# Transposing weights, queries and keys of a chunked-attention layer by 32x32 blocks and a trip through DRAM instead of by TensorE products

## The chip, the core and the metric

The kernel runs on one core of a Trainium2 chip. TensorE (PE) multiplies matrices, VectorE (DVE) and ScalarE (ACT) do the elementwise work, GpSimd (POOL) a few powers, and SyncE (SP) issues nearly all DMAs; 16 DMA engines move the bytes. The metric is device time in microseconds (us); lower is better. Each engine takes its instructions in the order in which the program lists them: an instruction that waits holds up those behind it on the same engine.

## What is computed

A model of four layers on 256 tokens of width 1024: a gated delta rule, an attention over one block, a retention layer, and, as the last, a chunked attention. Only the last, "layer D", is touched:

```python
proj = h @ w_in                                   # [256, 4 * 2048]
q, k, v, g = jnp.split(proj, 4, axis=-1)          # 16 heads of 128
q = rms_norm_f32(q.reshape(B, S, 16, 128), q_g)
k = rms_norm_f32(k.reshape(B, S, 16, 128), k_g)
...
s = einsum('bhqd,bhkd->bhqk', q_j, k_j) * scale + bias
p = softmax(where(valid, s, -1e30))
o = einsum('bhqk,bhkd->bqhd', p, v_j)
o = o * silu(g)
return o @ w_out
```

At 256 tokens each chunk of 64 queries sees all the chunks up to its own, so a head is one causal attention with a chunk-wise mask. All of it is float32.

## The kernel before

Weights come in units of [128, 1024] float32 (512 KB), one DMA each, into five `raw` buffers. ACT copies a unit to its first part `whi`, DVE subtracts it and gets the second part `wlo`; there are six pairs of parts. A product with split operands is three matmuls (hi·hi, hi·lo, lo·hi). `project_a` (L522) makes [128 tokens, 512 columns] twice, with four units of 12 matmuls of 512 columns; `project_b` (L501) makes [128 columns, 256 tokens] with a unit of 24 matmuls of 256 columns.

The order of the instructions is made on the host, when the program is built: `Tasks` (L269) runs each step of the work as a task with a priority, estimates what every operation takes, and issues the instructions in the order in which the engines would take them by these estimates. PE estimates are in `_cost_pe` (L237: 0.217 us for a split matmul of 512 columns); a DMA ends `DMA_LATENCY` = 2 us after its bytes have moved (L170, L353). On the chip, each engine then keeps that order, whatever things really take.

Layer D (`layer_d`, L1546) takes the units in the order `ORDER_D` (L157); q0 to q3 are the queries of four heads each, and so on for k, v and g (the gate); three gate units come ahead of all these. The pieces:

- `normed(name, q, reverse)` (L1590): after the projection, ACT squares and sums (eight instructions), POOL raises to the power -1/2, DVE scales into `xn` [128 tokens, 4 x 128]. For each half of the tokens PE then transposes four blocks of 128x128 by products with the identity (L1609), and ACT copies them to `qr` (reversed in order) or `kr`.
- `head(h)` (L1633) waits until its queries, keys, values and bias are there, then runs `attend` (L1108): scores on PE, softmax on DVE and ACT into `s`, three PE transposes of the weights (L1127), an ACT copy to `pT`, the product with the values, and an ACT copy to the output `or`. Heads have a priority (4.97) that goes before that of a projection (50 and more): their PE instructions are put between matmuls of projections as soon as the estimates have them ready.
- `gate(h)` (L1646) multiplies with 2 silu(g); `out_tile(n)` (L1679) makes 128 output columns each from 16 heads, adds them to `xT` and stores them.

PSUM has eight banks that the rings `PJ` (projections), `SS` (scores), `TT` (transposed weights), `OO` (outputs) and `MM` share. `hand_over(OO, TT)` (L1800) sets the shares of layer D: four for PJ, one each for SS, TT, OO and MM.

Of the kernel before, what the change touches and what calls it, by code (L numbers as in the profile page):

```python
# [10 lines left out]
F32 = mybir.dt.float32  # L11
# [9 lines left out]
P = 128  # L21
T = 256
D = 1024
# [3 lines left out]
# Per-partition columns: (name, number of columns)  # L27
# [12 lines left out]
# Constants that depend on shapes alone: (name, number of columns)  # L40
# [27 lines left out]
def _t5_hot():  # L68
    """[33, 384]: which bucket the relative position 255 - m falls in; the last row masks what lies ahead."""
    rel = 255 - np.arange(384)  # L70
    n = np.maximum(rel, 0)
    nf = np.maximum(n, 1).astype(np.float32)
    large = 16 + (np.log(nf / np.float32(16)) / np.float32(np.log(2048 / 16)) * np.float32(16)).astype(np.int32)
    bucket = np.where(n < 16, n, np.minimum(large, 31))
    hot = np.zeros((33, 384), np.float32)
    hot[bucket, np.arange(384)] = rel >= 0
    hot[32] = np.where(rel >= 0, 0.0, -1e30)
    return hot


def _decay():
    """[128 keys, 4 heads, 384]: key tile 0 with all queries, then key tile 1 with the last 128."""
# [29 lines left out]
def _plan():  # L112
    """The units of weights in the order of their use; those of the adaptive norms stand between the others."""
# [37 lines left out]
# Which units of weights are used whole, in float32 products  # L151
WHOLE = [("d_g", u) for u in (0,)] + [("a_qkv", u) for u in (0, 3, 4, 6, 7, 8, 9, 13, 14, 17, 18, 20, 22)]
# The order of the units
# [3 lines left out]
ORDER_D = "q1 k0 v0 q0 v2 g1 q2 k1 v1 q3 v3 g0 g3 k2 k3 g2".split()  # L157
ADA_FROM = ('a_z', 7)
ADA2_FROM = ('c_v', 3)
# Counts: units used before the norm, steps at once, units ahead, buffers  # L160
EARLY, BATCH, AHEAD, AHEAD2, FIRST_D, ADA_A, ADA2_EVERY = 1, 1, 1, 2, 3, 2, 1
RAWS, NPARTS, NKQ, NC, NVT = 5, 6, 3, 2, 2
# Priorities of tasks, the least goes first
# [4 lines left out]
# Estimates, in us  # L168
OVER, HOP, SAME = 0.03, 0.2, 0.1
DMA_LATENCY = 2.0  # L170
# [10 lines left out]
class Ring:  # L181
    """Free buffers: `b = yield ring` waits for one, ring.put(b) gives one back."""
# [22 lines left out]
class Engine:  # L205
    """Turns the calls of an engine into operations for a task to yield: (engine, estimated us, call, table)."""
# [57 lines left out]
def chain(*ops):  # L264
    """Operations of one engine, each on what the one before it made."""
    return [(e, c + SAME, f, t) for e, c, f, t in ops[:-1]] + [ops[-1]]


class Tasks:  # L269
    """Issues the instructions of concurrent tasks in the order in which the engines would take them.  # L270

    A task is a generator. It yields an operation or a list of operations of one engine, and goes on when they have
    ended by the estimates; a Ring, and gets a buffer; an Event, and waits for it; a number, its priority from there on
    (the least goes first)."""
# [59 lines left out]
    def dispatch(self, e):  # L334
# [18 lines left out]
        lat = DMA_LATENCY if e.startswith("D") else 0.0  # L353
# [5 lines left out]
        self.at(end + 1e-6, lambda: self.dispatch(e))  # the next operation of the same task may go first  # L359

    def hold(self, n):
        """While held, the vector and the scalar engine take nothing that can wait."""
        self.held += n
        if not self.held:
            for e in "VS":
                self.at(self.now, lambda e=e: self.dispatch(e))
# [10 lines left out]
def body(ctx, tc, a, out):  # L377
# [4 lines left out]
    dma, dma2 = Engine("D", nc.sync, _cost_dma), Engine("D2", nc.scalar, _cost_dma)  # L382

# [28 lines left out]
    nc.scalar.activation(phalf, nhalf, AF.Copy, scale=-1.0)  # the activation table is loaded meanwhile  # L412

    # PSUM: rings of whole banks; they change hands between the layers
# [22 lines left out]
    def h_set(i, name, wide=0):  # L437
        """Two float32r parts of transposed activations."""
# [10 lines left out]
    # ------------------------------------------------------------ weights: units of [128, 1024], in the order of use  # L449
# [11 lines left out]
    def unit(u):  # L461
        """One unit, whole or split exactly into two float32r parts; what belongs to the adaptive norms is summed at once."""
        raw = yield RAW
        src = a[u[0]][u[1]]
        if number[u] == 0:  # its first half is used before the other is there
# [35 lines left out]
    def project_b(units, x, x32, ps, ready):  # L501
        """[128 columns, tokens] of a product. x: (hi, lo) of the transposed activations, x32: the same, not split."""
# [19 lines left out]
    def project_a(name, q, x, pss, ready):  # L522
        """Two [128 tokens, 512 columns] of a product, with four units."""
# [32 lines left out]
    def sums_ops(ps, srcs):  # L556
        """Sums over the partitions of [128, 256] each, tokens on partitions: [128 tokens, 2, 96]."""
# [3 lines left out]
    def row_ops(ps, c):  # L561
        """A pair of token columns along the free dimension, on every partition."""
# [6 lines left out]
    # ------------------------------------------------------------ gated delta rule  # L569
    def layer_a(pool):  # L570
# [56 lines left out]
        def x_square(i):  # L627
            """Squares of two column tiles, added to those before."""
# [30 lines left out]
        def decays():  # L659
            """gg = -exp(a_log) softplus(a + dt_bias), beta = sigmoid(b), tokens on partitions"""  # L660
# [34 lines left out]
        def decay(h):  # L695
            """decay[s, c] = exp(sum of gg over s < m <= c), where the products of queries and keys will stand"""
# [16 lines left out]
        def conv(ch, dst):  # L713
            """dst [128, 256] = silu(conv) of channel tile ch."""
# [36 lines left out]
        def squared(h, x, dst):  # L751
            """Sums of the squares of the columns of x [128, 256]."""
# [7 lines left out]
        def norm_k(h, kq, done):  # L760
            """nk = the norm of the keys, bb = beta / nk ** 2"""
# [14 lines left out]
        def head(h):  # L776
            """The system matrices of head h and its squared norms."""
# [13 lines left out]
            # k.k of key tile 0 (256) and 1 (128), q.k of key tile 0 (256) and 1 (128)  # L791
# [10 lines left out]
            # the 16 x 16 diagonal blocks, side by side; then only what lies between blocks stays in MT  # L802
# [10 lines left out]
        def base(q):  # L813
            """V16 = (I + U)^-1 for the strictly upper 16 x 16 problems of four heads, block rows on partitions."""
# [31 lines left out]
        def gates(q):  # L846
            """zs = silu(z)"""
# [8 lines left out]
        # block solves: (I + B)^-1 = D (I - F)(I + F^2)(I + F^4), F = N D  # L856
# [54 lines left out]
        def outputs(t, q):  # L911
            """The outputs of four heads on one tile of tokens, their norm and gate, transposed in two parts."""
# [68 lines left out]
    def out_a(o_in, z_in, box, after):  # L981
        """The rows of the first four heads for all columns, then those of the others, two column tiles at a time."""
# [7 lines left out]
        # the two column tiles of a bank are one group, begun with zeros  # L990
# [35 lines left out]
    # ------------------------------------------------------------ from one layer to the next  # L1026
    class Next:
        """What the end of a layer makes for the next: scaled activations and sums of squares, a column tile at a time."""
# [24 lines left out]
        def squares(self, n):  # L1053
            """Adds to the sum; works on pairs, but for the last."""
# [22 lines left out]
        def weighted_squares(self, n, w):  # L1077
            """Adds to sums over the channels, tokens on partitions, with one weight of two for each half of the columns."""
# [11 lines left out]
    def ahead(u, nx, box):  # L1090
        """A product begun before its layer is, before norm and shift; box[u] = PSUM, with the product of the shift behind it."""
# [15 lines left out]
    # ------------------------------------------------------------ softmax attention of one head  # L1107
    def attend(A, kT, qT, bias, vv, o, half):  # L1108
        """o [128 dims, 256] = half times the output; queries stand reversed in their tile of 128 in qT and bias.

        x holds the negative scores, mx their least: minus the maximum of the scores."""
        ps = yield SS
        yield [pe.matmul(ps[:, :P], lhsT=qT[:, :P], rhs=kT[:, :P], start=True, stop=True),
               pe.matmul(ps[:, P:384], lhsT=qT[:, P:], rhs=kT, start=True, stop=True)]
# [11 lines left out]
        ps = yield TT  # L1126
        yield [pe.transpose(ps[:, i * P:(i + 1) * P], x[:, i * P:(i + 1) * P], ident) for i in range(3)]  # L1127
        A["s"].put(item)
        pT = yield A["pT"]
        yield s.activation(pT, ps[:, :384], AF.Copy)  # L1130
        TT.put(ps)
# [13 lines left out]
    def gate_out(o, zs, hi, lo):  # L1145
        """The two parts of o * zs."""
# [4 lines left out]
    # ------------------------------------------------------------ MoBA (one block of 256: causal attention within it)  # L1151
    def layer_b(pool, nx, begun, after):
# [16 lines left out]
        def biases():  # L1169
            """Rows of rel = 255 .. -127 for each head, then [128 - 1 - query, key]."""  # L1170
# [79 lines left out]
        def head(h):  # L1250
# [3 lines left out]
            yield from attend(A, K[h], Q[h], b_bias[:, h], [VV[q][:, t, hh * P:(hh + 1) * P] for t in range(2)], O[h], 1.0)  # L1254
# [43 lines left out]
    # ------------------------------------------------------------ adaptive norms  # L1298
    def cond(condb):
        """condb: silu(c) along the free dimension, on every partition"""  # L1300
# [4 lines left out]
    def ada(i, nx):  # L1305
        """mods[i] [128, 24]: shift, 1 + scale and gate of layer i as columns"""
# [11 lines left out]
    def modulate(hs, i, nx, k, r12, Y, r_in, done):  # L1318
        """hs = parts of rms_norm(x) * norm_g * (1 + scale) + shift"""
# [11 lines left out]
    def sixteen(pool, name, first):  # L1331
        """Two parts of [128, 16, 256], first: their first half."""
# [3 lines left out]
    # ------------------------------------------------------------ retention  # L1336
    def rope_tables(freq, sin, nsin, cos, done):
        """cos, sin and -sin of position * frequency, [128 frequencies, 256 tokens]"""
# [19 lines left out]
    def layer_c(pool, nx, first, sin, nsin, cos, rope_in, after, free):  # L1358
# [24 lines left out]
        def norm():  # L1383
            """The final norm (r1) and the norm of its result, together r12."""
# [501 lines left out]
```

## Time and profile before

| | us |
|---|---|
| median of 3 runs (801.78 to 802.7) | 802.01 |
| the profiled execution, its span | 799.7 |
| layer D from its first projection to the last matmul | 546.3 to 796.3 |
| PE busy over the span | 787.7 |
| DVE, ACT busy over the span | 566.3, 456.7 |

The span reaches from the first to the last instruction of one profiled execution; the 2.3 us between it and the median lie around it. A matmul's length in the profile overlaps with the next one's, since matmuls are pipelined; what a matmul costs is read from one start to the next. All times below count from the start of the span. Most instructions carry the line of the helper that issues them (L218), so groups are told apart by their tiles: `bank<-con,xn` is a transpose of `xn` by the identity (which lies in `con`), `bank<-con,s` one of softmax weights, `bank<-whi,hd_hi` a projection of layer D.

### The profile page before, as it was taken

The page shows a single profiled execution, that of the slowest core. Times are in us where ns is not written, and L with a number is a line of the kernel's source. Part 1 is how long each engine was busy: PE and PEld are TensorE (multiplying, and loading weights), DVE is VectorE, ACT ScalarE, POOL GpSimd, SP SyncE. Part 2 cuts the span into 40 slices and gives each one's busy share as a digit, 9 for nine tenths or more (in the row PEclk, how much of TensorE's full clock was granted, in tenths as well). Part 3 has the DMA queues.
Part 4 walks back from the last instruction along what each step waited for, and adds up shares of the span by engine and source line. Part 5 has one row for each costly group of instructions (what it writes and reads, how often), then busy time and mean ns, then how long its engine had stood idle before and what let it go on. Part 6 is the DMA issues. An engine that isn't in the chain of part 4 may idle for free.

```text
span 799.7 us, 13581 instructions
## 1 busy us (share of the span) xinstructions
PE 787.7 (98%) x5117; PEld 710.3 (89%) x5117; DVE 566.3 (71%) x1157; ACT 456.7 (57%) x968; POOL 37.6 (5%) x45
## 2 busy tenths in 40 slices
PE   6999999999999999999999999999999999999998
PEld 5898889989899999998888879998889888989998
DVE  5799998346997978698467889768547556557751
ACT  4886453545635786644445454655657567558740
POOL 0120100010000000000000000000100000000000
PEclk9999999999999999999999999999999999999999
DMA  8536443125768866728558899865654665564340
GB/s 286 181 106 210 133 143 120 55 80 174 254 219 324 296 218 203 239 77 286 158 142 275 304 309 325 259 185 191 211 177 128 209 181 151 171 187 132 103 132 27
DMA packets 45946, 151.15 MB, mean 189 GB/s; under 512 B 5135, under 2 KB 10040, under 8 KB 45880
## 3 DMA queue, kind: packets, MB, share of 16 engines
q1 hardware_dynamic: 44824, 149.22, 57.9%
q10 hardware_dynamic: 1056, 1.06, 0.5%
q8 instruction: 40, 0.66, 0.3%
q14 instruction: 26, 0.21, 0.1%
HBM read 149.20 MB, written 1.06 MB: 188 GB/s over the span
## 4 chain that ended last, share of the span: by engine, by line
PE 98%; DMA 1%; DVE 0%; ACT 0%; issue 0%; POOL 0%; SPq 0%; DVEq 0%
PE bank L218 98%; DMA xT<-in_xT 1%; ACT js L218 0%; POOL rs L218 0%; DVE r L218 0%; DVE hi L218 0%; ACT r L218 0%; DVE xT L218 0%; DVE lo L218 0%; ACT rsrow L218 0%; SPq L218 0%; DVE rs L218 0%; ACT whi L218 0%; DVEq L218 0%
## 5 line engine op out<-in xcount | busy, mean ns | idle before, releaser
L218 ACT ACTIVATE whi<-raw 128x1024 fp32r<-128x1024 f32 x210 | 222.2, 1060 | 200.8 <-PE bank L218 168.5
L218 DVE TENSOR_TENSOR wlo<-raw,whi 128x1024 fp32r<-128x1024 f32 x210 | 256.0, 1223 | 104.9 <-ACT whi L218 103.8
L218 PE MATMUL bank<-whi,hd_hi 128*128 128x512 f32 x192 | 78.0, 406 | 0.0
L218 PE MATMUL bank<-wlo,hd_hi 128*128 128x512 f32 x192 | 75.7, 394 | 0.0
L218 PE MATMUL bank<-whi,hd_lo 128*128 128x512 f32 x192 | 75.6, 394 | 0.0
L218 DVE CUSTOM_DVE_ANT_0 raw<-raw,condb 128x1024 f32<-128x1024 f32 x48 | 58.5, 1220 | 8.9 <-DMA raw<-in_ada 8.8
L218 PE MATMUL bank<-whi,hc_hi 128*128 128x512 f32 x128 | 52.0, 406 | 0.0
L218 PE MATMUL bank<-whi,hc_lo 128*128 128x512 f32 x128 | 50.5, 395 | 0.0
L218 PE MATMUL bank<-wlo,hc_hi 128*128 128x512 f32 x128 | 50.4, 394 | 0.0
L218 PE MATMUL bank<-lo,raw 128*128 128x256 f32 x192 | 44.3, 379 | 0.9 <-DVE lo L218 0.9
L218 PEld LDWEIGHTS bank<-whi,hd_lo 128*128 128x128 f32 x192 | 36.2, 188 | 8.6
L218 PEld LDWEIGHTS bank<-whi,hd_hi 128*128 128x128 f32 x192 | 36.1, 188 | 7.4
L218 PEld LDWEIGHTS bank<-wlo,hd_hi 128*128 128x128 f32 x192 | 36.2, 188 | 7.4
L218 PEld LDWEIGHTS bank<-lo,raw 128*128 128x128 f32 x192 | 35.1, 189 | 5.4 <-DVE lo L218 1.1
L218 PE MATMUL bank<-hb_hi,whi 128*128 128x256 f32 x128 | 38.4, 300 | 0.0
L218 PE MATMUL bank<-hb_hi,wlo 128*128 128x256 f32 x128 | 36.3, 283 | 0.0
L218 PE MATMUL bank<-hb_lo,whi 128*128 128x256 f32 x128 | 36.1, 282 | 0.0
L218 PE MATMUL bank<-hd_hi,whi 128*128 128x256 f32 x104 | 31.7, 305 | 0.0
L218 PE MATMUL bank<-ha_hi,whi 128*128 128x256 f32 (+1 forms) x96 | 29.5, 307 | 0.0
L218 PE MATMUL bank<-hd_hi,wlo 128*128 128x256 f32 x104 | 29.3, 282 | 0.0
L218 PE MATMUL bank<-hd_lo,whi 128*128 128x256 f32 x104 | 29.3, 282 | 0.0
L218 PEld LDWEIGHTS bank<-whi,hc_lo 128*128 128x128 f32 x128 | 24.1, 188 | 5.7
(322 smaller groups left out, 2157.3 us busy)
## 6 DMA issues: line engine op xcount, KB each, us to landing
raw<-in_ada SPq DMA_DIRECT2D x48, 512.0 KB, 4.6
raw<-in_a_qkv SPq DMA_DIRECT2D x23, 512.0 KB, 4.6
raw<-in_c_v SPq DMA_DIRECT2D x16, 512.0 KB, 4.3
raw<-in_c_g SPq DMA_DIRECT2D x16, 512.0 KB, 4.0
raw<-in_c_out SPq DMA_DIRECT2D x16, 512.0 KB, 4.9
raw<-in_d_g SPq DMA_DIRECT2D x16, 512.0 KB, 3.7
raw<-in_d_q SPq DMA_DIRECT2D x16, 512.0 KB, 3.6
raw<-in_d_k SPq DMA_DIRECT2D x16, 512.0 KB, 3.6
```

The costliest lines, as they stand in the source:

```text
L218: return self.key, c, lambda: f(*a, **k), func and func.name
```

## The change

Layer D alone no longer transposes on PE. DVE transposes every 32x32 block in place of its 128x128 tile (`v.transpose`), a DMA writes the result to DRAM in runs of 512 bytes (`turn_out`), and four DMAs, one for each group of 32 partitions, read it back in runs of 128 bytes (32 numbers), so that the blocks change places (`turn_in`). The DMAs are issued on SP, between the loads of weights; the host's plan counts them on a queue of their own ("DB") with 0.45 us each and 4 us from there to their end. For keys the last read lands in `kr` itself; for queries it lands in `QT`, and ACT copies it reversed, 1024 columns at once. The weights of a head are read back straight into `pT`.

Buffers: `ZX` (two halves of `condb`) and `A["z"]`, `QT` (parts of the `x32` tile, free once the activations of layer D are made) hold what goes out and comes in. PSUM: there is no TT in layer D and SS gets its bank, so two heads can have scores at once; the bank of MM goes to PJ after the norm, which makes five. `ORDER_D` is another. Layer B, which uses `attend` too, keeps its products with the identity.

```diff
-ORDER_D = "q1 k0 v0 q0 v2 g1 q2 k1 v1 q3 v3 g0 g3 k2 k3 g2".split()
+ORDER_D = "q1 k1 q0 v1 k0 v0 q2 g1 k2 v2 q3 k3 g0 v3 g2 g3".split()
-DMA_LATENCY = 2.0
+LATENCY = {"D": 2.0, "D2": 2.0, "DB": 4.0}
...
+    turn = Engine("DB", nc.sync, lambda *x: 0.45)
...
+    def turn_out(z, d):
+        return turn.dma_start(out=bass.AP(tensor=d.tensor, offset=d.offset, ap=[[P, P], [P * P, z.shape[1] // P], [1, P]]),
+                             in_=z.rearrange("p (m c) -> p m c", c=P))
+
+    def turn_in(dst, d):
+        n = dst.shape[1] // 32
+        return [turn.dma_start(out=dst[32 * b:32 * b + 32].rearrange("j (m i) -> j m i", i=32),
+                              in_=bass.AP(tensor=d.tensor, offset=d.offset + 32 * b, ap=[[P, 32], [32 * P, n], [1, 32]]))
+                for b in range(4)]
...
     def attend(A, kT, qT, bias, vv, o, half):
...
-        ps = yield TT
-        yield [pe.transpose(ps[:, i * P:(i + 1) * P], x[:, i * P:(i + 1) * P], ident) for i in range(3)]
-        A["s"].put(item)
-        pT = yield A["pT"]
-        yield s.activation(pT, ps[:, :384], AF.Copy)
-        TT.put(ps)
+        if "z" not in A:
...
+        else:
+            z = yield A["z"]
+            yield v.transpose(z, x)
+            A["s"].put(item)
+            d = tc.dram_tile([3, P, P], F32, name="p_d")
+            yield turn_out(z, d)
+            A["z"].put(z)
+            pT = yield A["pT"]
+            yield turn_in(pT, d)
...
     def normed(name, q, reverse):
...
+            d = tc.dram_tile([8, P, P], F32, name=name + "_d")
             for t in range(2):
                 xn = yield XN
                 yield v.tensor_mul(xn, pss[t].rearrange("p (h d) -> p h d", h=4), f[:, t, :, None].to_broadcast([P, 4, P]))
                 PJ.put(pss[t])
-                ps = yield MM
-                yield [pe.transpose(ps[:, hh * P:(hh + 1) * P], xn[:, hh], ident) for hh in range(4)]
+                z = yield ZX
+                yield v.transpose(z, xn.rearrange("p h d -> p (h d)"))
                 XN.put(xn)
...
+                yield turn_out(z, d[4 * t:4 * t + 4])
+                ZX.put(z)
+            if reverse:
+                tmp = yield QT
+                yield turn_in(tmp, d)
+                yield qkg_in
+                yield s.activation(dst.rearrange("p t h i -> p (t h) i")[:, :, ::-1],
+                                   tmp.rearrange("p (m i) -> p m i", i=P), AF.Copy, scale=qkg)
+                QT.put(tmp)
+            else:
+                yield turn_in(dst.rearrange("p t h i -> p (t h i)"), d)
...
-        yield from hand_over(OO, TT)
+        yield from hand_over(OO, SS)
```

## Rows read from the trace of the kernel before

**Rows 1.** The page: the span, the engines, the chain that ended last
```profile
span 799.7 us, 13581 instructions
PE 787.7 (98%) x5117; PEld 710.3 (89%) x5117; DVE 566.3 (71%) x1157; ACT 456.7 (57%) x968; POOL 37.6 (5%) x45
...
PE 98%; DMA 1%; DVE 0%; ACT 0%; issue 0%; POOL 0%; SPq 0%; DVEq 0%
```

**Rows 2.** Stretches of layer D: busy us (count), granted clock, DMA share, GB/s
```profile
546.30:600.00 53.70, 53.70 (x242) 43.68 (x241) 32.38 (x45) 32.06 (x80) 5.20 (x4) 1.00 0.59 180
...
546.30:797.00 250.70, 250.13 (x1514) 222.08 (x1512) 144.62 (x279) 145.68 (x357) 14.27 (x11) 1.00 0.50 151
```

**Rows 3.** Waits from 546.3 to 797: us in total, times, longest
```profile
ACT whi L218 <- PE bank L218: 58.8, 46, 1.8
...
SPq L218 <- DVE wlo L218: 136.7, 53, 9.9
```

**Rows 4.** Groups of instructions by shape, 546.3 to 797: PE, DVE and ACT
```profile
L218 PE MATMUL bank<-con,xn 128*128 128x128 f32 x64 | 9.6, 273 | 0.0
L218 PE MATMUL bank<-con,s 128*128 128x128 f32 x48 | 7.9, 273 | 0.0
...
L218 DVE TENSOR_TENSOR xn<-bank,fr 128x512 f32<-128x512 f32 x16 | 10.9, 683 | 0.2 <-POOL fr L218 0.2
L218 DVE TENSOR_SCALAR s<-s,sm 128x256 f32<-128x256 f32 x16 | 5.6, 347 | 0.0
...
L218 ACT ACTIVATE pT<-bank 128x384 f32<-128x384 f32 x16 | 7.8, 489 | 1.2 <-PE bank L218 1.1
L218 ACT ACTIVATE kr<-bank 128x512 f32<-128x512 f32 x8 | 4.8, 598 | 6.6 <-PE bank L218 6.6
```

**Rows 5.** Timeline of PE (start, us, operation): transposes of xn between projections
```profile
564.58 0.39 PE L218 MATMUL bank<-wlo,hd_hi 128*128 128x512 f32 x1
564.81 0.40 PE L218 MATMUL bank<-whi,hd_lo 128*128 128x512 f32 x1
565.05 0.60 PE L218 MATMUL bank<-con,xn 128*128 128x128 f32 x4
565.41 0.48 PE L218 MATMUL bank<-whi,hd_hi 128*128 128x512 f32 x1
565.73 0.39 PE L218 MATMUL bank<-wlo,hd_hi 128*128 128x512 f32 x1
```

**Rows 6.** Timeline of PE: transposes of softmax weights between gate projections
```profile
610.38 0.28 PE L218 MATMUL bank<-hd_hi,wlo 128*128 128x256 f32 x1
610.50 0.49 PE L218 MATMUL bank<-con,s 128*128 128x128 f32 x3
610.74 0.37 PE L218 MATMUL bank<-hd_hi,whi 128*128 128x256 f32 x1
610.95 0.28 PE L218 MATMUL bank<-hd_lo,whi 128*128 128x256 f32 x1
```

**Rows 7.** Stretches with one load of weights, and with one store, alone
```profile
634.30:637.00 2.70, 2.70 (x13) 2.19 (x13) 1.23 (x1) 2.70 (x18) 0.00 (x0) 1.00 0.52 194
791.90:792.80 0.90, 0.90 (x9) 0.90 (x9) 0.00 (x0) 0.00 (x0) 0.00 (x0) 1.00 0.43 146
```

**Rows 8.** Timeline of ACT's and SP's queues: a trip through DRAM; the length of issues
```profile
191.23 0.55 ACTq L218 DMA_DIRECT2D ext_d<-s  x1
193.10 0.40 ACTq L218 DMA_DIRECT2D b_bias<-ext_d  x1
...
541.02 0.43 SPq L218 DMA_DIRECT2D br<-in_d_rel  x1
```

**Rows 9.** DMA issues: operation, count, KB each, median us from issue to landing
```profile
raw<-in_d_q SPq DMA_DIRECT2D x16, 512.0 KB, 3.6
br<-in_d_rel SPq DMA_DIRECT2D x4, 512.0 KB, 5.0
out<-xT SPq DMA_DIRECT2D x8, 128.0 KB, 2.9
```

More of the change, by code (lines that the diff above doesn't have):

```diff
@@ L352, in dispatch @@
         self.free[e] = end
-        lat = DMA_LATENCY if e.startswith("D") else 0.0
+        lat = LATENCY.get(e, 0.0)
         def ended():
@@ L1105, in begin @@
         return box
+    def turn_out(z, d):
[6 more added lines that the diff above has]
+                for b in range(4)]
     def attend(A, kT, qT, bias, vv, o, half):
         ps = yield SS
-        yield [pe.matmul(ps[:, :P], lhsT=qT[:, :P], rhs=kT[:, :P], start=True, stop=True),
-               pe.matmul(ps[:, P:384], lhsT=qT[:, P:], rhs=kT, start=True, stop=True)]
+        yield [pe.matmul(ps[:, :P], lhsT=qT[:, 0], rhs=kT[:, 0], start=True, stop=True),
+               pe.matmul(ps[:, P:384].rearrange("p (t i) -> p t i", t=2), lhsT=qT[:, 1], rhs=kT, start=True, stop=True)]
         x, mx, sm = item = yield A["s"]
@@ L1125, in attend @@
                for t, sl in enumerate(cut)]
-        ps = yield TT
-        yield [pe.transpose(ps[:, i * P:(i + 1) * P], x[:, i * P:(i + 1) * P], ident) for i in range(3)]
-        A["s"].put(item)
-        pT = yield A["pT"]
-        yield s.activation(pT, ps[:, :384], AF.Copy)
-        TT.put(ps)
+        if "z" not in A:
+            ps = yield TT
+            yield [pe.transpose(ps[:, i * P:(i + 1) * P], x[:, i * P:(i + 1) * P], ident) for i in range(3)]
+            A["s"].put(item)
+            pT = yield A["pT"]
+            yield s.activation(pT, ps[:, :384], AF.Copy)
+            TT.put(ps)
+        else:
+            z = yield A["z"]
+            yield v.transpose(z, x)
+            A["s"].put(item)
+            d = tc.dram_tile([3, P, P], F32, name="p_d")
+            yield turn_out(z, d)
+            A["z"].put(z)
+            pT = yield A["pT"]
+            yield turn_in(pT, d)
         ps = yield OO
@@ L1253, in head @@
                 yield e
-            yield from attend(A, K[h], Q[h], b_bias[:, h], [VV[q][:, t, hh * P:(hh + 1) * P] for t in range(2)], O[h], 1.0)
+            yield from attend(A, *(x.rearrange("p (t i) -> p t i", t=2) for x in (K[h], Q[h])), b_bias[:, h], [VV[q][:, t, hh * P:(hh + 1) * P] for t in range(2)], O[h], 1.0)
             run.set(o_in[h])
@@ L1552, in layer_d @@
         A = attend_rings(pool, 3)
+        A["z"] = Ring(run, [])
         m, rs, r12, qkg = buf("m", [P, 2]), buf("rs", [P, 2]), buf("r12", [P, T]), buf("qkg", [P, 1])
+        ZX = Ring(run, [late["condb"][:, i * 512:(i + 1) * 512] for i in range(2)])
         hs = h_set(0, "hd")
@@ L1556, in layer_d @@
         Y, XN, FR = Ring(run, [r.free[0][:, i] for r in SQ for i in range(2)]), ring(pool, "xn", [P, 4, P], 3), Ring(run, [(buf(f"ms{i}", [P, 2, 4]), buf(f"fr{i}", [P, 2, 4])) for i in range(2)])
-        QR, KR, VR = (ring(pool, n, [P, 4, 2, P], 2) for n in ("qr", "kr", "vr"))
+        QR, KR, VR = (ring(pool, n, x, 2) for n, x in (("qr", [P, 2, 4, P]), ("kr", [P, 2, 4, P]), ("vr", [P, 4, 2, P])))
+        QT = Ring(run, [])
         BR, OR, ZR = ring(pool, "br", [P, 4, T], 2), ring(pool, "or", [P, T], 5), ring(pool, "zr", [P, T], 5)
@@ L1574, in norm @@
             yield v.tensor_copy(r12, ps[:, :T])
-            MM.put(ps)
+            PJ.put(ps)
             run.set(r12_in)
@@ L1607, in normed @@
                 PJ.put(pss[t])
-                ps = yield MM
-                yield [pe.transpose(ps[:, hh * P:(hh + 1) * P], xn[:, hh], ident) for hh in range(4)]
+                z = yield ZX
+                yield v.transpose(z, xn.rearrange("p h d -> p (h d)"))
                 XN.put(xn)
-                x = ps.rearrange("p (h i) -> p h i", h=4)
-                if reverse:
-                    yield qkg_in
-                    yield s.activation(dst[:, :, t, ::-1], x, AF.Copy, scale=qkg)
-                else:
-                    yield s.activation(dst[:, :, t], x, AF.Copy)
-                MM.put(ps)
+                yield turn_out(z, d[4 * t:4 * t + 4])
[9 more added lines that the diff above has]
+                yield turn_in(dst.rearrange("p t h i -> p (t h i)"), d)
             FR.put(item)
@@ L1637, in head @@
             o = O[h] = yield OR
-            yield from attend(A, K[q][:, hh].rearrange("p t i -> p (t i)"), Q[q][:, hh].rearrange("p t i -> p (t i)"),
+            yield from attend(A, K[q][:, :, hh], Q[q][:, :, hh],
                               B[q][:, hh], [VV[q][:, hh, t] for t in range(2)], o, 0.5)
@@ L1688, in out_tile, with more @@
             yield dma.dma_start(out=out[:, n], in_=xT[:, n])
+        def more():
+            for e in hs_in + [first["in", ("d_g", u)] for u in range(FIRST_D)]:
+                yield e
+            x = x32_tile("zd", 2).rearrange("p k t -> p (k t)")
+            for i in range(2):
+                A["z"].put(x[:, i * 384:(i + 1) * 384])
+            QT.put(x[:, 1024:2048])
+        run.spawn(more(), 1)
         run.spawn(norm(), 2)
```

## The prediction

> **What bounds the kernel now.** I read the page first: PE is busy for 98% of the span and makes up 98% of the chain that ended last [rows 1]. An average can hide a stage with another limit, so I cut layer D into stretches: PE is busy for 53.70 of 53.70 us while projections run, at the full granted clock of 1.00, and over the whole layer for 250.13 of 250.70 us [rows 2]. PE waits for nothing in the layer that the change touches. So the time falls by what leaves PE and rises by every wait that PE gets. The others have room: DVE and ACT work for 145 and 146 of the 250.7 us, the DMA engines for 0.59 of the time where projections run [rows 2]. The weights are ahead of PE: ACT's longest waits before it splits a unit are for PE, which must free a pair of parts (58.8 us), and SP's are for a raw buffer (136.7 us) [rows 3].
>
> **What leaves PE.** Matmuls overlap, so the busy times of the groups (9.6 and 7.9 us [rows 4]) are not what PE gets back; starts are. Two neighbouring projection steps take 0.23 us each (564.58 to 564.81). With four transposes of xn between them, the way from 564.81 to the second step behind, 565.73, takes 0.92 instead of 0.46: 0.46 us for four [rows 5]. There are 64 [rows 4], so 16 x 0.46 = 7.4 us. Between gate steps of 0.12 us, three transposes of weights stretch 610.38 to 610.95 from 0.24 to 0.57: 0.33 us for three [rows 6]. There are 48 [rows 4], so 16 x 0.33 = 5.3 us. Together 12.7 us; I count 12.5, as some places beside other short matmuls will give less. More can't come from PE, and nothing is added to it. Its reordered units are the same products.
>
> **What goes to DVE and ACT.** DVE gets 16 transposes of 512 columns and 16 of 384; none is in the trace. The nearest rows are 683 ns for 512 columns and 347 for 256 columns [rows 4]. I take 0.65 and 0.5 us, 18 us in all (16 to 36, if an element costs up to twice that). They lie in DVE's 106 us of idle time. ACT loses the copies to `kr` and `pT`, 4.8 + 7.8 us [rows 4]; the copies to `qr` stay, wider. Neither is on PE's path: nothing. The PSUM banks that change hands cost and give nothing, since PE waits for no bank now.
>
> **What goes to the DMA engines.** Out go 8 x 512 KB of queries and keys and 16 x 192 KB of weights, 7.3 MB in 14,336 runs of 512 bytes; back they come in 57,344 runs of 128 bytes. A run's price I take from two transfers alone: a load of 128 runs of 4 KB is 0.52 of 2.70 us on 16 engines, 175 ns a run; a store of 128 runs of 1 KB is 0.43 of 0.90 us, 48 ns [rows 7]. A line through both gives 27 ns at 512 bytes and 11.5 at 128. The bounds for 128 bytes are 11.5 (the line) and 48 (no cheaper than the nearest row). I take 11.5 because the two rows show that time goes with bytes. Then the trips take (57,344 x 11.5 + 14,336 x 27) / 16 = 41 + 24 = 65 us of all 16 engines. They fall into some 185 us (546 to about 731); a unit's load takes 175 x 128 / 16 = 1.4 us in each 2.8 us of PE time, which leaves about 90 us free. So the engines go to 0.85: they hold the traffic, but queue.
>
> **What goes to SP.** 32 stores and 96 reads, 128 issues at 0.43 us [rows 8], 55 us; SP idles 137 us for raw buffers [rows 3], which hides them. The reads wait on SP until the store has landed, and loads of weights are queued behind them. The full pairs of parts cover this: about five units of 2.8 us. If that cover goes, PE waits for weights directly.
>
> **The round trips against the plan.** This is what decides. PE's order is fixed by the plan: a product with weights (16 heads) or with keys is put at the place at which the plan has the trip done, and if the trip is longer, PE stands. The plan gives it 0.45 + 4 us out and 4 x 0.45 + 4 us in, 10.25 us. The plan also takes PE for faster than it is (0.217 us for a step that takes 0.23 [rows 5]), some 7%, so that the chip has about 11 us. The trip of weights: a store of 192 KB lies between 128 KB in 2.9 and 512 KB in 512 runs in 5.0 us [rows 9], say 3.3. Of four reads the last is issued 1.4 us after the first [rows 8] and lands 2.9 us later [rows 9], with 0.5 for what is left of its data: 4.8. Together 8.1 us if the queues are empty. The small trip in this trace bears this out from below: 12 KB to DRAM, and 1.9 us later the read is issued [rows 8]. Each half can meet a load of weights, up to 2.2 us, 0.65 on average at 0.6 busy: 9.4, at worst 12.5. So a head's trip mostly fits; I take 0.4 us of waits for each. The heads go in pairs (two buffers of `A["z"]`), eight pairs: 3 us (0 to 12). Keys: a store of 256 KB takes 3.6, the reads of 4,096 runs 4,096 x 11.5 / 16 = 2.9 us of data and 2.9 to land: 9.4, with queueing 10.7 to 13.8. Where a group's values come soon behind its keys, PE meets this: heads 0 to 3, 8 to 11 and 12 to 15 of the new order; in the first, q0 and v1 (22 us) lie between k1 and the heads. 1 us each: 3 us (0 to 8).
>
> **The end.** Behind k3 stand one gate unit, v3, g2 and g3, 2.9 + 11.1 + 11.4 + 11.4 = 37 us (0.23 us a step of 512 columns, 0.12 a step of 256 [rows 5, 6]), and heads on top, some 10 us. The keys need some 20 us, four heads some 20 more. The output tiles then want the last heads. A margin of 5 to 8 us: nothing, but it is gone if trips are 6 us longer.
>
> **Sum.** The profiled execution: 799.7 - 12.5 + 3 + 3 = 793.2 us of span; the median lies 2.3 us above the span, so 802.0 - 6.5 = 795.5 us.
>
> **Rivals.** (A) All trips fit, and PE gets back everything: 802.0 - 12.5 = 789.5 us. For it: the plan has 2.2 us to spare on an empty queue. Against: the queue will not be empty. (B) Slower: trips outlast the plan by more than I think. With a lateness d for a pair of heads, the wait comes at eight pairs, and about as often again as trips hold buffers and keys come late: about 8 d in all. At d = 1.6 us the gain is gone; at d = 3 us it is +24 - 12.5, 813 us. For it: a busy share of 0.85, and a median of 5.0 us for the only transfer of 512 runs [rows 9], for which the plan's formula would give 3.6. (C) Slower: short runs cost more than the line says and the DMA engines become the bound. It decides at (90 - 24) x 16 / 57,344 = 18 ns a run. At 27 ns, the price of a 512-byte run, the trips take 97 + 24 = 121 us, 31 more than is free: 802 + 31 - 12.5 = 820 us. At 48 ns it would be 196 us and about 895. Nothing in this trace moves many runs of 128 bytes, so only the line speaks against it. The Trainium skill has a rule on this side: its page "VectorE: DVE Perf Modes", section "The three transpose paths", calls a plain DMA copy that transposes by its access pattern a trap, 19x slower than the crossbar's transpose; and "DMA: Bandwidth & Descriptors", section "Specifications", wants 512 bytes for line rate. The blocks of 32 are what avoids single numbers here, and no run here shows the rule yet; by it the outcome is (C). (D) That it doesn't do what it says has no room: the products with the identity of layer D go, those of layer B stay and are not counted.
>
> **How the numbers follow.** The forecast, 790.5 to 800.4: 0.43. (A), below: 0.17. Within 0.2% (800.4 to 803.6, about what a measurement can tell from no change), when waits eat the gain: 0.12. Slower: 0.28, of which (B) 0.16 and (C) 0.12. Faster by over 0.2% is then 0.60. The range goes from 789, the whole gain, to 815, which takes in (B) at d = 3 and leaves out most of (C), 0.12, and 0.05 below.
>
> **What would show it.** After: no group of `con,xn` or `con,s` in layer D; the steps between projections at 0.23 without gaps. Waits of PE on the DMAs to `pT` and `kr` are the 6 us: near none means (A), 1.5 us and more per pair means (B). For (C) the DMA share would be at 0.95 and above from 565 to 730 and ACT would wait for raw buffers to land instead of for PE. Landing times of the reads above 6 us for `pT` or 8 for `kr` would make the prediction wrong.

## The result: 0.55% slower, because TensorE now waits

The changed kernel takes 806.54 us (median of 7 runs, 803.81 to 810.19) where the kernel before takes 802.60 beside it: a ratio of 1.0055, interval 1.0036 to 1.0073. I had forecast 795.5 us, faster. The time lies inside the range, on the other side of no change.

The page of the changed kernel, the lines that answer to [rows 1], and the DMA packets:

```profile
span 803.2 us, 13599 instructions
PE 779.2 (97%) x5005; PEld 698.6 (87%) x5005; DVE 581.1 (72%) x1189; ACT 443.5 (55%) x940; POOL 37.3 (5%) x45
...
DMA packets 119675, 165.83 MB, mean 206 GB/s; under 512 B 64527, under 2 KB 83768, under 8 KB 119608
...
PE 83%; DMA 9%; DVE 3%; SPq 3%; issue 1%; ACT 1%; POOL 0%; ACTq 0%; DVEq 0%
```

PE has 112 instructions fewer, as intended, and 8.5 us less busy time. But the chain that ended last, which was PE for 98%, now leaves PE for 17% of the span: DMA, DVE and SP's queue stand in it. (That is the path of the chain, not time in which PE stands; PE's waits are counted below.) Stretches of layer D (columns as in [rows 2]):

```profile
547.50:600.00 52.50, 49.69 (x218) 39.88 (x216) 35.12 (x52) 30.63 (x77) 5.21 (x4) 1.00 0.74 206
600.00:650.00 50.00, 44.79 (x237) 37.58 (x236) 29.48 (x67) 27.59 (x76) 3.58 (x3) 1.00 0.98 238
650.00:700.00 50.00, 48.15 (x227) 39.54 (x226) 34.03 (x71) 28.17 (x75) 3.58 (x3) 1.00 0.95 252
700.00:750.00 50.00, 48.17 (x318) 43.75 (x318) 37.65 (x90) 31.29 (x81) 1.64 (x1) 1.00 0.88 218
750.00:800.00 50.00, 49.98 (x411) 49.38 (x409) 22.68 (x34) 15.05 (x23) 0.00 (x0) 1.00 0.52 127
```

PE is no longer busy throughout, and the share of the DMA engines between 600 and 700 goes to 0.98 and 0.95. In the kernel before the same stretches read:

```profile
600.00:650.00 50.00, 50.00 (x288) 43.65 (x287) 28.39 (x59) 33.45 (x85) 2.64 (x3) 1.00 0.56 168
650.00:700.00 50.00, 50.00 (x293) 43.77 (x292) 30.47 (x61) 31.62 (x72) 3.16 (x3) 1.00 0.57 167
```

The waits can be seen one by one. This is PE's timeline at the first product with read-back weights; a step of 0.23 us becomes one of 2.45:

```profile
617.38 0.39 PE L218 MATMUL bank<-whi,hd_hi 128*128 128x512 f32 x1
617.61 0.39 PE L218 MATMUL bank<-wlo,hd_hi 128*128 128x512 f32 x1
617.84 0.40 PE L218 MATMUL bank<-whi,hd_lo 128*128 128x512 f32 x1
620.29 0.89 PE L218 MATMUL bank<-pT,vr 128*128 128x256 f32 x4 [2.05 <-DMA pT<-p_d]
```

I measured each such step from one start to the next, less the usual step, from 547 us to the end, and took those over 0.35 us: eleven, 13.5 us in all. Five stand before a product with weights (5.7 us), four before a product with keys (4.9 us), two before a projection (2.9 us). The kernel before has none. PE's own table of waits counts less, since it counts from the end of the matmul before (617.84 + 0.40 for the one above) and not from the usual next start (617.84 + 0.23), but it has the same names:

```profile
PE bank L218 <- DMA pT<-p_d: 4.6, 4, 2.0
PE bank L218 <- DMA kr<-d_k_d: 2.9, 3, 1.6
PE bank L218 <- ACT vr L218: 2.3, 1, 2.3
```

So in the profiled execution layer D lasts 252.2 us from the first projection's start to the last matmul's, against 249.9 before, 2.3 us more. Without its waits it would last 238.7 us, 11.2 less than before: that is what PE got back. Counted by the number of transposes it should be 12.3 us (112 at 0.11 us from start to start); the other 1.1 us are the rest of this sum, spread over small steps, and I did not trace them. The layer starts 1.2 us later than before; in the experiments it starts anywhere from 546.5 to 547.8, so I don't put that down to the change. This execution's time is 805.03 us. The median is another 1.5 us higher: of the seven executions the two at a mean granted clock of 1.000 took 803.8 and 805.0 us, the five at 0.994 to 0.998 took 805.9 to 810.2. The fourth experiment shows what such a clock can come from.

### The profile page after: what moved, and what is told of

Same layout as the page of the kernel before. It is cut to its first block, busy times and chain, and to the rows that moved or that the text cites. A ratio compares the mean times of both kernels' runs of the same rounds, so it can differ in the third digit from the quotient of the medians.

```text
span 803.2 us, 13599 instructions
## 1 busy us (share of the span) xinstructions
PE 779.2 (97%) x5005; PEld 698.6 (87%) x5005; DVE 581.1 (72%) x1189; ACT 443.5 (55%) x940; POOL 37.3 (5%) x45
## 4 chain that ended last, share of the span: by engine, by line
PE 83%; DMA 9%; DVE 3%; SPq 3%; issue 1%; ACT 1%; POOL 0%; ACTq 0%; DVEq 0%
PE bank L218 83%; DMA pT<-p_d 3%; SPq L218 3%; DMA d_k_d<-condb 3%; DMA kr<-d_k_d 2%; DVE wlo L218 1%; DMA raw<-in_a_qkv 1%; DMA raw<-in_a_z 1%; ACT whi L218 1%; DVE s L218 1%; DVE condb L218 0%; ACT xn L218 0%; DVE xn L218 0%; DVE zd L218 0%; ACT qr L218 0%
```

## Where a trip loses its time

SP's queue of the changed kernel around the first two heads (start, length, DMA):

```profile
604.34 0.38 SPq L218 DMA_DIRECT2D d_q_d<-condb  x1
605.59 1.41 SPq L218 DMA_DIRECT2D p_d<-zd  x2
608.75 0.34 SPq L218 DMA_DIRECT2D raw<-in_d_g  x1
609.20 3.80 SPq L218 DMA_DIRECT2D zd<-d_q_d  x4
613.05 0.87 SPq L218 DMA_DIRECT2D raw<-in_d_g  x1
613.96 1.97 SPq L218 DMA_DIRECT2D pT<-p_d  x4
616.03 0.41 SPq L218 DMA_DIRECT2D raw<-in_d_g  x1
616.49 2.92 SPq L218 DMA_DIRECT2D pT<-p_d  x4
619.74 0.38 SPq L218 DMA_DIRECT2D p_d<-zd  x1
```

The first head's weights are stored at 605.59. Their reads are issued at 613.96, since two loads and the reads of the queries stand ahead, and these reads alone take 3.8 us to issue; the product starts at 620.29, 14.7 us after the store where the plan has 10.25. The third head's weights were transposed at 610.41 but stored only at 619.74: on SP the store stands behind the reads of the queries and of both heads ahead of it. From 609.20 to 619.74 SP hardly waits: it is issuing for 10.0 of these 10.5 us. Over the 16 heads, from the end of the transpose to the start of the product, the median is 14.5 us (10.95 to 21.3). Of this, 7.7 us (4.0 to 14.0) pass before the first read is issued, 1.7 from the first read's issue to the last's. What makes the queue slow is that an issue is longer (tile views; ns min/median/max):

```profile
L218 SPq DMA_DIRECT2D pT<-p_d x64: 302/462/2068, 614.0 to 765.5; - x64
L218 SPq DMA_DIRECT2D kr<-d_k_d x16: 325/558/2793, 592.9 to 736.9; - x16
L218 SPq DMA_DIRECT2D zd<-d_q_d x16: 320/700/4295, 579.0 to 726.8; - x16
```

The issue of 0.43 us [rows 8] is up to ten times as long, and the 128 issues of all trips take SP 78 us instead of the 55 that I had counted. The landing times are nearer to what I took, 4.8 us for a read of weights where I had 3.4 (us from issue to landing, last column):

```profile
raw<-in_d_q SPq DMA_DIRECT2D x16, 512.0 KB, 4.2
...
p_d<-zd SPq DMA_DIRECT2D x16, 192.0 KB, 3.4
pT<-p_d SPq DMA_DIRECT2D x64, 48.0 KB, 4.8
...
d_k_d<-condb SPq DMA_DIRECT2D x8, 256.0 KB, 5.4
...
kr<-d_k_d SPq DMA_DIRECT2D x16, 128.0 KB, 4.0
```

## The experiments

Each was run beside the kernel before; the ratios are to that. "Waits" are PE's steps over 0.35 us too long in the profiled execution, as above. Two theories to begin with: L, the DMA engines are full and this makes trips late; S, a single trip is longer than planned even without load. Later a third, O: SP's one order.

**One part alone: weights (e1_heads).** `normed` transposes on PE as before; `attend` is that of the change, the order is the new one.

```diff
             for t in range(2):
...
-                z = yield ZX
-                yield v.transpose(z, xn.rearrange("p h d -> p (h d)"))
+                ps = yield MM
+                yield [pe.transpose(ps[:, hh * P:(hh + 1) * P], xn[:, hh], ident) for hh in range(4)]
```

> Only the softmax weights go through DRAM; queries and keys are transposed on PE again, in the new order. PE gets back 5.3 us instead of 12.7. Theory L (load: trips last longer than planned because the DMA engines are full, a share of 0.95 to 0.98): with 24,576 short reads instead of 57,344 the trips come near the plan, the waits of PE for the weights fall from 5.7 us to 1 to 2 us, 799 us. Theory S (single trips: even alone a trip of weights takes 3 us more than the plan gives it): the 5.7 us of waits stay, 803 us.

Measured: 798.73 us, ratio 0.9946 (0.9929 to 0.9962). Waits 2.0 us, one of 1.55 on `pT`. With this part alone the DMA engines are less busy:

```profile
600.00:650.00 50.00, 50.00 (x283) 43.45 (x282) 32.99 (x79) 32.64 (x94) 3.58 (x3) 1.00 0.81 206
650.00:700.00 50.00, 50.00 (x238) 41.43 (x237) 33.45 (x74) 30.82 (x82) 3.58 (x3) 1.00 0.82 212
```

The same 16 trips that cost 5.7 us of waits in the full change cost 1.6 here, as L says. S falls as the whole story. But SP also has 48 DMAs fewer to issue here, so this run does not tell full engines from a full queue on SP; e5_long takes that up. The kernel is faster than the kernel before and than the change.

**The other part alone: queries and keys (e2_qk).** `attend` without the trip (no `A["z"]`), `hand_over(OO, TT)` as before.

> Only queries and keys go through DRAM; the softmax weights are transposed on PE again. PE gets back 7.4 us. In the changed kernel the waits on this part were 4.9 us for keys and 2.4 us for a PSUM bank that ACT freed late because it waited for queries. Theory L: less load, waits 2 to 4 us, 798 us. Theory S: waits 7.3 us stay, 802.6 us.

Measured: 800.59 us, ratio 0.9973 (0.9962 to 0.9984). Waits 5.1 us: 2.2 for the PSUM bank behind ACT, 2.9 before keys. Between the two expectations: the share of DMA is 0.79 to 0.83 here, and keys wait for less (2.9 instead of 4.9), but the bank behind ACT as long. The two parts alone gain 3.8 and 1.9 us on the kernel before; together they lose 3.9. They share something.

**The order alone (e3_order).** The kernel before with the new `ORDER_D`.

> The kernel before with the new order of units alone, everything transposed on PE. All theories on trips: no wait of PE, 802.6 us within 1 us. If the order itself costs or gives something (values and keys that come later, a fuller end), the time moves by more than 2 us.

Measured: 803.26 us, ratio 1.0008 (0.9999 to 1.0018); waits 0.5 us. The order by itself is nothing.

**The plan (e4_plan55).**

```diff
-LATENCY = {"D": 2.0, "D2": 2.0, "DB": 4.0}
+LATENCY = {"D": 2.0, "D2": 2.0, "DB": 5.5}
```

> The changed kernel with one number of the plan changed: a trip's DMA ends 5.5 us after its issue instead of 4.0, 3 us more for both halves, so PE's products are put later between the projections. If the waits come from a plan that is too short by a few us (S, and L as far as the queue stays as it is): waits fall from 13.5 us to 4 to 6 us, 797 to 799 us. If the DMA engines or SP's queue can't move the traffic of a group of heads in time (capacity), later places help little: 804 to 806 us.

Measured: 804.54 us, ratio 1.0027 (1.0008 to 1.0045). Waits 8.6 us, less than 13.5, but of those that remain two are longer than any before, 2.5 and 2.9 us, and the time is nearly that of the change. All ten executions had a mean granted clock of 0.992 to 0.998. The profiled one shows why; stretches around a wait, and one behind the other long wait, which ends at 729.3:

```profile
628.00:633.00 5.00, 5.00 (x35) 4.56 (x34) 2.87 (x3) 3.88 (x12) 0.00 (x0) 1.00 1.08 291
633.70:636.30 2.60, 0.27 (x3) 0.06 (x1) 2.07 (x4) 1.51 (x5) 1.64 (x1) 1.00 0.91 226
637.60:641.10 3.50, 3.50 (x17) 3.32 (x17) 1.74 (x3) 0.72 (x3) 0.00 (x0) 0.52 0.90 289
641.20:646.00 4.80, 4.80 (x43) 4.80 (x42) 2.53 (x4) 2.97 (x5) 0.00 (x0) 1.00 0.97 225
...
730.00:733.00 3.00, 3.00 (x16) 3.00 (x15) 0.85 (x2) 0.80 (x2) 0.00 (x0) 0.50 1.01 293
```

PE stands still from 633.7 to 636.3, and from 637.6 to 641.1 the granted clock is 0.52, the lower of its two levels (1.2 GHz) but for the edges. A gate step takes 0.21 us there instead of 0.12, which costs 3.5 x (1 - 0.12/0.21) = 1.5 us. The same follows the wait of 2.9 us. These two waits thus cost about their length and half again, and with some 3 us for both stretches the 4.9 us of waits saved shrink to the 2.0 us by which layer D is shorter here. It is no rule: in e11_headsk, below, a wait of 2.6 us is followed by a clock of 1.00 throughout. In the profiled execution of the change no wait was over 2.45 us and no stretch of this kind appears; that the executions of the change with a lower mean clock had one is likely, but no trace of them shows it. (The share of the DMA engines can read above 1.00, as in the first row, so a share near 1.00 is not by itself proof that they are full.)

**Long runs (e5_long).** The reads take whole rows, without the exchange of the blocks.

```diff
-        n = dst.shape[1] // 32
-        return [turn.dma_start(out=dst[32 * b:32 * b + 32].rearrange("j (m i) -> j m i", i=32),
-                              in_=bass.AP(tensor=d.tensor, offset=d.offset + 32 * b, ap=[[P, 32], [32 * P, n], [1, 32]]))
+        n = dst.shape[1]
+        return [turn.dma_start(out=dst[32 * b:32 * b + 32],
+                              in_=bass.AP(tensor=d.tensor, offset=d.offset + 32 * n * b, ap=[[n, 32], [1, n]]))
                 for b in range(4)]
```

> The changed kernel, but each read takes whole rows in a row (runs of 1.5 KB for weights, 4 KB for queries and keys) instead of runs of 128 bytes; bytes, DMAs, issues, waits and order are the same. It leaves out the exchange of the blocks, so its numbers are not the layer's. Theory L (the DMA engines are full of short runs): the share of the DMA engines in 600 to 700 falls from 0.95 to 0.98 to about 0.75, issues on SP no longer last up to 4 us, the waits of PE fall from 13.5 to 2 to 4 us: 792 to 794 us. Theory O (what counts is SP's one queue, in which stores and reads stand behind each other's waits and behind loads): most waits stay, 800 to 804 us.

Measured: 795.89 us, ratio 0.9926 (0.9904 to 0.9947). Waits 5.8 us instead of 13.5; PE's largest, and two stretches:

```profile
PE bank L218 <- DMA pT<-p_d: 1.4, 2, 1.2
PE bank L218 <- ACT whi L218: 1.1, 1, 1.1
PE bank L218 <- ACT vr L218: 1.0, 1, 1.0
```

```profile
600.00:650.00 50.00, 47.04 (x255) 39.75 (x254) 32.59 (x69) 28.59 (x75) 3.58 (x3) 1.00 0.79 234
650.00:700.00 50.00, 49.54 (x228) 40.70 (x227) 35.55 (x81) 29.81 (x81) 3.58 (x3) 1.00 0.86 250
```

Nothing differs but the length (and so the number) of the runs, and 10.7 us of the median go, and 7.7 us of waits in the profiled executions. So the short runs are the larger half of the matter. They act on SP's queue as well: the 128 issues of the trips take 53 us here instead of 78. The other 5.8 us of waits stay with the short runs gone; neither L nor O had it alone.

**Long runs and the later plan (e8_long55).** The two edits together.

> The reads in long runs once more (without the exchange of the blocks), and the plan gives a trip's DMA 5.5 us instead of 4.0. With long runs alone 5.9 us of waits were left at a share of 0.79 to 0.87. If those were a plan too short by a few us: waits of 1 to 2 us, 791 to 793 us. If they come from SP's one queue, in which trips hold each other up whatever the plan says: 795 to 796 us as with 4.0.

Measured: 794.22 us, ratio 0.9892 (0.9880 to 0.9905). Waits 1.8 us, one only, the bank behind ACT; none over 0.35 us on a trip. The profiled execution has a span of 790.5 us, 9.2 less than before; as in e5_long the exchange of the blocks is left out, so this is no time of the layer. The waits are as expected from the plan; the time is a little over the 791 to 793 us, and less than 2 us under e5_long, about what the intervals can tell. So with engines that have room, the waits on trips that are left come from a plan too short by a few us, and the plan can mend them; with short runs (e4_plan55) the same number took away 4.9 of 13.5 us and left 6.9 before weights.

**Another queue (e7_poolq).** Stores and reads on GpSimd: `turn = Engine("DB", nc.gpsimd, ...)`.

> The changed kernel with the stores and reads of the trips issued by GpSimd instead of SP, which keeps the loads of weights: the traffic is the same, but the trips wait no longer behind loads that wait for a raw buffer. Theory O: waits fall to half, 798 to 800 us, if GpSimd makes its descriptors as fast as SP. Theory L: the engines are as full as before, 804 to 807 us; above 812 us if GpSimd needs several us for the 4,096 runs of a read.

Measured: 823.74 us (818.18 to 830.84), ratio 1.0242 (1.0201 to 1.0283). Waits some 24 us, with one of 5.6 and one of 4.2, and 24 us, 3% of the span, at the lower clock. Two views of what GpSimd adds:

```profile
L218 POOL DMA_DIRECT2D pT<-p_d x64: 616/617/654, 615.4 to 783.8; - x64
...
DVE xn L218 <- POOL fr L218: 10.0, 4, 3.5
```

An issue takes 0.62 us for each of 64, 0.75 and more for the others, 90 us for all 128 where SP takes 78 in the change. And GpSimd also makes the powers of the norms, which stand behind the trips: DVE waits 10.0 us for them here and never in the change. How the 17 us of loss divide between the two is not shown. This doesn't separate O from L: the new queue is slower than the old one, and has other work. How much of a trip's lateness is SP's order alone stays open.

**The copy behind the reads (e6_pool).** What the prediction did not see: the ACT copy to `qr` waits for the reads, and ACT takes nothing meanwhile. In the changed kernel:

```profile
588.54 1.15 ACT L218 ACTIVATE qr<-zd,qkg 128x1024 f32<-128x1024 f32 x1 [3.64 <-DMA zd<-d_q_d]
...
592.53 2.05 ACT L218 ACTIVATE whi<-raw 128x1024 fp32r<-128x1024 f32 x2
594.43 1.13 ACT L218 ACTIVATE vr<-bank 128x512 f32<-128x512 f32 x2
```

PE's wait from 592.45 to 595.12 ends with this `vr`, which frees a bank; ACT is 3.6 us late from the wait for the queries. The edit puts the copy on GpSimd:

```diff
-                yield s.activation(dst.rearrange("p t h i -> p (t h) i")[:, :, ::-1],
-                                   tmp.rearrange("p (m i) -> p m i", i=P), AF.Copy, scale=qkg)
+                yield g.tensor_scalar(out=dst.rearrange("p t h i -> p (t h) i")[:, :, ::-1],
+                                      in0=tmp.rearrange("p (m i) -> p m i", i=P), scalar1=qkg, scalar2=None, op0=ALU.mult)
```

> The changed kernel with the copy of the read-back queries on GpSimd instead of ACT. In the changed kernel ACT waits 6.4 us for these reads, and behind it stand the copies of values that free PSUM banks for projections; PE's longest wait, 2.4 us at 592.5, ended with such a copy. If that is its cause, this wait goes and with it the half-clock stretch that such a wait can bring: 802 to 804 us. If the bank was late for another reason: no change, 806.5 us.

Measured: 808.86 us, ratio 1.0075 (1.0055 to 1.0095). The wait at 592 is gone, so its cause is right; but there are waits of 5.1 and 4.8 us now, before weights and before keys. GpSimd holds still for the reads:

```profile
POOL qr L218 <- DMA zd<-d_q_d: 67.7, 4, 22.6
```

Behind the copy stand the powers (`fr`) of the keys and queries that follow. But most of this time GpSimd has nothing else to do: of these powers only one starts right behind a copy (669.10), the others come after a wait for DVE's sums. The two long waits have another cause, on SP's queue; ahead of the second, which ends at 735.9:

```profile
723.49 4.74 SPq L218 DMA_DIRECT2D zd<-d_q_d  x4
728.28 3.69 SPq L218 DMA_DIRECT2D kr<-d_k_d  x4
```

The reads of the keys stand behind four reads of queries, and the eight take 8.4 us to issue. Ahead of the first, too, reads of queries (4.2 us of issue at 615.21) and loads stand before the reads of the head's weights at 622.76. My expectation had moved a wait and not asked what comes late next.

**Weights and queries (c9_headsq), weights and keys (e11_headsk).** The first has the copy on GpSimd, as in e6_pool; keys, or queries, are transposed on PE.

> Weights and queries through DRAM, keys transposed on PE, the copy of queries on GpSimd. PE gets back 5.3 + 3.7 = 9.0 us; 41,000 short reads. If load and waits grow in proportion (2 us of waits with the weights alone, 13.5 with all): waits 5 to 6 us, 798 to 800 us, no better than the weights alone. If the keys, which heads wait for, were most of the trouble: waits 2 to 3 us, 795 to 796 us.

Measured: 805.65 us, ratio 1.0054 (1.0033 to 1.0076), waits 8.4 us. That is above both expectations. The two largest waits are 3.4 us before weights, whose reads stand on SP behind 5.4 us of issuing reads of queries, and 2.6 us before a projection at 570, which has to do with no trip (as in the next run). GpSimd waits 43.3 us for the reads here, but neither of these two waits ends with it.

> Weights and keys through DRAM, queries transposed on PE: no copy waits for a read on any engine. PE gets back 5.3 + 3.7 = 9.0 us, 41,000 short reads. If a share of 0.85 or more is what makes trips late: waits 4 to 6 us, 799 us or more. If the copy of the queries behind its read was what made the trouble: waits 2 us, 795 to 796 us.

Measured: 804.80 us, ratio 1.0033 (1.0014 to 1.0052), waits 9.4 us: 4.2 before weights, 1.9 before keys, 3.3 before projections. No copy waits for a read in this kernel, so that copy was not most of the trouble. The share of DMA is 0.85 to 0.87 in 600 to 700. The waits are above the 4 to 6 us that I expected from the load. The 2.6 us before a projection at 581 end with DVE's scaling of `xn`, which frees the bank:

```profile
582.09 1.23 DVE L218 TENSOR_TENSOR wlo<-raw,whi 128x1024 fp32r<-128x1024 f32 x1 [1.50 <-ACT whi L218]
583.23 0.68 DVE L218 TENSOR_TENSOR xn<-bank,fr 128x512 f32<-128x512 f32 x1
```

In DVE's order the scaling stands behind a subtraction that waits for ACT's copy, and ACT had waited 1.7 us for PE to free a pair of parts. No trip is in it, so it belongs to the order of this kernel; without it 6.8 us are left.

**The order again, with trips (e10_heads_old).** e1_heads with the order before.

> Only the weights through DRAM, with the order of units before. In the order before, the last heads need k3, after which only one gate group stands, so four heads' trips have 11 us of projections to lie beside instead of 23. If the new order is what hides the last trips: several us of waits before the output tiles, 803 to 806 us. If the order does not matter: 799 us.

Measured: 809.19 us, ratio 1.0082 (1.0069 to 1.0095); e1_heads took 798.7. The order that does nothing alone is worth 10 us once heads have trips: waits 7.4 us, 4.8 of them at 684 to 691, where two pairs of heads follow each other with no projections between, the rest at the end before the output tiles. From 687.4 on PE has the lower clock for 6.8 us (0.50 in 688 to 694), which costs up to 3.4 us more.

**The best found (e9_heads55).** Only the weights through DRAM, 5.5 us in the plan.

> Only the weights through DRAM (798.7 us, 2.0 us of waits left), with 5.5 us in the plan. If the plan was what was left: no waits, 797 us. If the later places open new gaps at the end: 799 us or more.

Measured: 797.91 us, ratio 0.9949 (0.9932 to 0.9966), 4.1 us faster than the kernel before and 8.6 faster than the change. Waits 0.6 us, none on a trip. It differs from e1_heads (798.73) by less than the intervals can tell.

```profile
600.00:650.00 50.00, 50.00 (x285) 43.61 (x283) 33.15 (x76) 32.73 (x91) 3.58 (x3) 1.00 0.78 202
650.00:700.00 50.00, 50.00 (x236) 41.35 (x235) 34.12 (x74) 31.07 (x84) 3.58 (x3) 1.00 0.87 215
```

## Why the prediction was wrong, point by point

- **What leaves PE** was right but for 1.3 us: 12.5 us forecast, 11.2 in PE's starts without the waits. In e9_heads55, where PE hardly waits, the weights' share of 5.3 us comes back as 4.1 (by the ratio) to 4.7 us (by the medians).
- **DVE and ACT.** A transpose takes 570 ns for 384 columns and 708 for 512, against 500 and 650: 20 us of DVE, off the path, as said.
- **The DMA engines' price was too low.** Over layer D their share goes from 0.50 of 250.7 us [rows 2] to 0.82 of 249.5, so 125 us become 205. I had 65 us more, it is 79. With the stores as I priced them (24 us), 55 are left for 57,344 reads, an estimate of 15 ns each instead of 11.5. That is below the 18 ns from which rival C decides, so C did not come about. But 0.85 became 0.95 to 0.98 between 600 and 700 us, where eight of the 16 heads lie. The Trainium skill, page "DMA: Bandwidth & Descriptors", section "Specifications", asks for 512 bytes for line rate; the rows agree in direction: 128 bytes in 15 ns are 8.5 GB/s an engine, 4 KB in 175 ns are 23. The 19x that the prediction took from the Trainium skill, page "VectorE: DVE Perf Modes", section "The three transpose paths", is against the crossbar's transpose, which no run here has. What the runs show is that the short runs cost the larger half of the waits, and not what (C) forecast.
- **The step that failed is the round trips against the plan.** I took 9.4 us for a trip of weights and 0.4 us of waits for each; up to the start of the product the median is 14.5, and the waits are 5.7 us instead of 3 with weights, 4.9 instead of 3 with keys. Landing times were the smaller part (3.4 for the store and 4.8 for a read, against 3.3 and 3.4), and the sign that I had named, landings of `pT` above 6 us, did not show in the median. The larger part is what passes before the first read is issued: 7.7 us where I had 3.3 for the store, or 4.0 with a load in the way. (For the 2.2 us of such a load I gave no row; by [rows 7] a load alone takes 0.52 x 2.70 = 1.4.) What I left out was SP: I counted what its issues take (55 us, hidden in its idle time; they took 78) and who waits behind them among the loads, but not that one trip's reads stand ahead of the next trip's store, nor that an issue of short runs can last up to 4.3 us.
- **A wait that I didn't list**: ACT for the queries, 6.4 us in three waits, with the copies that free PSUM banks queued behind it. I had put ACT's part at nothing, since it only lost work. It cost PE 2.4 us, and e2_qk has it as well. The longest issue stands in this wait: the third of the four reads of these queries was issued from 580.41 to 584.70.
- **The price of a wait of PE** was its length. Behind the waits of 2.5 and 2.9 us of e4_plan55 the rows show stretches at the lower clock, some 1.5 us more each.
- **Rival B** was the outcome: its account of eight lateness units d gives d = (806.5 - 802.6 + 12.5) / 8 = 2.1 us. Its way of counting was not borne out: five of the 16 heads made PE wait for weights, not eight pairs evenly. I had given it 0.16, on a queue that I had worked out to be at 0.85.

The span of the change's profiled execution, in terms: 799.7 - 11.2 + 13.5 of waits + 1.2 of the later start = 803.2. Of the 1.5 us from this execution's time to the median I know only that the slower executions had the lower mean clock.

## What to carry to other kernels

Work taken off the bounding engine comes back as waits where its result must now arrive by a fixed place: price the whole way, with each queue's order, and not only the transfers. When several such ways share one in-order queue and one set of DMA engines, try each part alone, and stop before the way is full: here the two parts gained 3.8 and 1.9 us alone and lost 3.9 together. A wait put on another engine can come back elsewhere; ask what comes late next.

## What the hardware showed that I had not expected

- A DMA's issue on SP, 0.33 to 0.43 us in the kernel before, lasts up to 4.3 us for a read of 1,024 runs of 128 bytes (median 0.70 for these; 0.42 and at most 0.58 with the same bytes in long runs, in e5_long).
- In e4_plan55 the two standstills of PE of 2.5 and 2.9 us were each followed by a stretch at the lower granted clock (0.52 from 637.6 to 641.1; 0.50 from 730 to 733), after PE had resumed; a wait of 2.6 us in e11_headsk was not.
- An issue of a trip's DMA on GpSimd takes 0.62 to 0.79 us (medians), and moving the trips there made the kernel some 2% slower than the change.
